# The first scale's weights by columns, and three conv tiles that run ahead of the shift

## The chip, the cores and the metric

One core of a Trainium2 chip runs the whole program once. The metric is the device time of that core in microseconds (us). PE is TensorE, DVE is VectorE, ACT is ScalarE, POOL is GpSimd, SP issues most of the transfers. A MiB is 128 partitions x 2048 fp32 words, the size of one weight tile.

## The reference

A decoder trunk of two layers over 256 tokens of width 1024. Only the head of its first layer matters here:

```python
c_act = jax.nn.silu(c)
sh1, sc1, g1, sh2, sc2, g2 = jnp.split(c_act @ ada_w[l] + ada_b[l], 6, axis=-1)
h = x * (1.0 + sc1[:, None, :]) + sh1[:, None, :]
# conv_module
a, g = jnp.split(h @ w_in + b_in, 2, axis=-1)
u = a * jax.nn.sigmoid(g)
u = depthwise_causal_conv(u, w_dw, taps=31) + b_dw
u = jax.nn.silu(layer_norm(u, g_n, b_n))
return u @ w_out + b_out
```

After it come the channel mixer (SwiGLU), the shared K/V projection, block-sparse attention and a mixture of eight experts, which make up most of the time and are not touched.

## The kernel before

Every fp32 product is made of three: each factor is split into a high and a low part (fp32r), and `mm3` (L198) adds high x high, high x low and low x high in PSUM. A weight tile is loaded (`load`, L165), its high part made by ACT (L189) and its low part by DVE, or by POOL for the names in `SPLIT_POOL` (L190).

The shift and the scale of the first layer are the two halves of one group of `ada_w`, `e00`. Each half is a product of the one row `c_act` (copied 32 times, `crep`) with a 1024x1024 matrix, in four row tiles of 1 MiB: `e00_w00` to `e00_w03` for the shift, `e00_w10` to `e00_w13` for the scale (`Ada.step`, L227). The result lies in rows, gets its bias from a broadcast load (`e00_b0`, L255), an add (L258), two transposes (L266) and a copy (L267), and is then a column per channel block: `c00c` for the scale, `c00h` for the shift.

The conv input projection has eight tiles of 256 output columns, `ci0` to `ci7`, in the order gate, value, gate, value; their PSUM tiles are `cip`. The program runs so:

- The scale half of `e00` and then `x` (token-major) are loaded; PE transposes `x` (`x_tr`, L325). `modulate` (L332) makes `hs` = x (1 + scale), without the shift, as a high and a low part.
- The first two tiles (`FIRST = 2`) multiply `hs`. What the shift adds to them is made separately: `shw` = shift x weights, 32 products into two rows (L519), copied (`shr`, L522), turned into columns by eight tiny products (L526) and added to the bias as `cin` (L530).
- The other six tiles multiply `h` = x (1 + scale) + shift (`hT`), made by a second `modulate`.
- From each pair of tiles ACT takes the sigmoid (`sg`, L588) and DVE makes `U` (L591), two blocks of 128 channels.
- The 31 taps of the eight channel blocks are divided: `CONV_VECTOR` on DVE (L548, five blocks and parts), `CONV_POOL` on ACT and POOL (blocks 1 and 3 whole and a part of 5: ACT multiplies, `pr`, L561, and POOL adds, L562, 70 adds), `CONV_TENSOR` on PE with diagonal matrices (`dg`, L476). DVE adds the parts of shared blocks (`dw`+`cp`, L612).
- The four tiles of the output projection, `cout`, have their low parts made by POOL (L190), behind its 70 adds. Then come the norm (L630 to L662) and the rest.

The order on each engine is that of a scheduler with a timeline of its own, which takes the program's instructions and their dependences; each engine's queue then runs in that order. SP's queue is the order of the loads.

Of the kernel before, what the change touches and what calls it, by code (L numbers as in the profile page):

```python
# [19 lines left out]
P = 128  # L20
D = 1024
# [50 lines left out]

CONV_VECTOR = (((0, 0, CK), (2, 0, CK)), ((4, 0, CK), (5, 11, CK), (7, 27, CK)))
FIRST = 2
SPLIT_POOL = ("ci2_0", "ci4_0", )
LN_ADD = ((1, 1),)
# [6 lines left out]
def build(ctx: ExitStack, tc: tile.TileContext, a: dict, dbg: dict | None = None):  # L85
# [92 lines left out]

    def split(raw, shape, name, spare=False, parts=1, gates=(), sub=None):
# [321 lines left out]
    wfirst = []
    for t in range(FIRST):
        if t:
            e00.fetch(0, 3)
        wfirst += colchunk(win, in_cols(t), 256, f"ci{t}", parts=1 if t else 2)
    c00h = ada_cols(e00.done(0), "c00h", sideps)
# [4 lines left out]
    psfirst = []  # L511
    for t in range(FIRST):
        psfirst.append(mmps(f"cip{t}"))
        dmajor([psfirst[-1]], wfirst[t:t + 1], hs)
# [12 lines left out]
    cin = small.tile([P, FIRST, 2], F32, tag="cin", name="cin", bufs=1)
# [56 lines left out]
    for ch in range(4):  # L584
# [701 lines left out]
```

## Time and profile before

| | |
|---|---|
| median of 3 runs | 1528.99 us (1527.67 to 1530.91) |
| the profiled execution | 1529.28 us |
| its span, first to last instruction | 1527.6 us |
| PE busy | 1469.6 us, 96% |
| DVE / ACT / POOL busy | 83% / 64% / 7% |
| granted TensorE clock, mean | 0.983 |

Busy time and spans are those of one profiled execution. The rows below show an engine's instructions in order of time: the start, the time from there to the end of the row's last instruction, the engine, the line, the output and its inputs, the shapes, how many, and in brackets how long the engine was idle before and what ended that. A clock of 1.00 is 2.4 GHz, 0.5 is 1.2 GHz.

### The profile page before, as it was taken

Reading aid. Unit: us, or ns where it says so; the run is one execution under the profiler, and the core shown is the slowest. Engines: PE = TensorE matmul, PEld = TensorE weight load, DVE = VectorE, ACT = ScalarE, POOL = GpSimd, SP = SyncE. Lnnn points to the kernel's source line nnn. Section 1 sums busy time; section 2 is a strip of 40 time slices with the busy share of each in tenths; the row PEclk is TensorE's granted clock in tenths of the full one; section 3 lists DMA queues with packets and bytes.
Section 4 is the critical chain, followed back from the end, with each engine's and each line's share of the span. In section 5 each row is a group of like instructions: output and inputs, shape, how many; then the busy total and the mean of one; then the engine's idle time right before and its main releaser. Section 6 shows DMA issues by size and latency. Waiting matters only on the chain. (4 is left out here: it accounts for less than half of the span.)

```text
span 1527.6 us, 20443 instructions
## 1 busy us (share of the span) xinstructions
PE 1469.6 (96%) x8042; PEld 1210.3 (79%) x8042; DVE 1264.0 (83%) x1260; ACT 985.0 (64%) x949; POOL 104.2 (7%) x101
## 2 busy tenths in 40 slices
PE   5995999999999999999999999999999999999995
PEld 3883798998976787888888888888888888887884
DVE  2897677756777799899889899988989988988886
ACT  5665444434656577777776776777767777667673
POOL 0696100001000100000000000000000000000000
PEclk9997999999999899999999999999999999999998
DMA  9765588865972688999999999999999999999991
GB/s 358 294 252 213 206 337 310 323 244 218 367 256 105 257 308 330 375 364 358 352 355 347 366 359 366 339 361 370 349 381 367 336 347 374 346 380 340 349 363 64
DMA packets 73380, 484.51 MB, mean 317 GB/s; under 512 B 9044, under 2 KB 11452, under 8 KB 17468
## 3 DMA queue, kind: packets, MB, share of 16 engines
q1 hardware_dynamic: 72848, 482.94, 84.1%
q8 instruction: 65, 1.06, 0.3%
q14 instruction: 39, 0.32, 0.1%
q10 hardware_dynamic: 428, 0.18, 0.0%
HBM read 482.04 MB, written 1.05 MB: 316 GB/s over the span
## 5 line engine op out<-in xcount | busy, mean ns | idle before, releaser
L190 DVE TENSOR_TENSOR eu_l<-eu,eu_h 128x2048 fp32r<-128x2048 f32 (+1 forms) x233 | 508.1, 2204 | 42.8 <-ACT eu_h L189 42.2
L189 ACT ACTIVATE eu_h<-eu 128x2048 fp32r<-128x2048 f32 (+1 forms) x233 | 425.7, 1848 | 100.4 <-PE eup L201 64.2
L202 PE MATMUL eup<-eu_l,g_x 128*128 128x512 f32 x896 | 353.8, 397 | 1.1 <-DVE eu_l L190 0.8
L200 PE MATMUL eup<-eu_h,g_x 128*128 128x512 f32 x896 | 350.4, 391 | 1.8 <-ACT eu_h L189 1.8
L201 PE MATMUL eup<-eu_h,g_x 128*128 128x512 f32 x896 | 349.8, 390 | 0.0
L190 DVE TENSOR_TENSOR e_l<-e,e_h 128x2048 fp32r<-128x2048 f32 (+1 forms) x114 | 251.0, 2212 | 25.8 <-ACT e_h L189 25.6
L189 ACT ACTIVATE e_h<-e 128x2048 fp32r<-128x2048 f32 (+1 forms) x114 | 210.2, 1854 | 21.5 <-PE eup L201 19.4
L202 PEld LDWEIGHTS eup<-eu_l,g_x 128*128 128x128 f32 x896 | 168.2, 188 | 43.2 <-DVE eu_l L190 9.5
L200 PEld LDWEIGHTS eup<-eu_h,g_x 128*128 128x128 f32 x896 | 168.3, 188 | 36.0 <-ACT eu_h L189 2.9
L201 PEld LDWEIGHTS eup<-eu_h,g_x 128*128 128x128 f32 x896 | 168.2, 188 | 35.7
L201 PE MATMUL eo<-e_h,egt 128*128 128x512 f32 x440 | 171.9, 391 | 0.0
L200 PE MATMUL eo<-e_h,egt 128*128 128x512 f32 x440 | 171.5, 391 | 0.0
L202 PE MATMUL eo<-e_l,egt 128*128 128x512 f32 x440 | 156.4, 397 | 0.0
L200 PEld LDWEIGHTS eo<-e_h,egt 128*128 128x128 f32 x440 | 82.6, 188 | 18.3 <-ACT e_h L189 0.4
L201 PEld LDWEIGHTS eo<-e_h,egt 128*128 128x128 f32 x440 | 82.6, 188 | 17.4
L202 PEld LDWEIGHTS eo<-e_l,egt 128*128 128x128 f32 x440 | 79.8, 188 | 15.5 <-issue 0.5
L1031 ACT ACTIVATE egt<-ept 128x512 fp32r<-128x512 f32 x56 | 33.2, 592 | 85.7 <-PE ept L1027 85.7
L1058 POOL TENSOR_TENSOR e_last_l<-e_last,e_last_h 128x1024 fp32r<-128x1024 f32 x1 | 3.0, 2994 | 988.3 <-ACT e_last_h L1056 988.3
L1023 ACT ACTIVATE es<-eup 128x512 f32<-128x512 f32 x56 | 33.3, 594 | 42.2 <-PE eup L202 41.9
L562 POOL TENSOR_TENSOR dw<-dw,pr 128x256 f32<-128x256 f32 x70 | 56.8, 814 | 5.1
L1024 DVE TENSOR_TENSOR eg<-es,eup 128x512 f32<-128x512 f32 x56 | 38.2, 683 | 17.6 <-PE eup L202 17.6
L227 PE MATMUL e_ps<-e_w,crep 128*32 128x256 f32 x576 | 43.8, 444 | 6.6 <-DMA e_w<-in_stream_dram 6.0
(400 smaller groups left out, 2424.1 us busy)
## 6 DMA issues: line engine op xcount, KB each, us to landing
eu<-in_stream_dram SPq DMA_DIRECT2D x216, 1024.0 KB, 6.8
e<-in_stream_dram SPq DMA_DIRECT2D x106, 1024.0 KB, 7.0
e_w<-in_stream_dram SPq DMA_DIRECT2D x46, 1024.0 KB, 6.1
fa<-in_stream_dram SPq DMA_DIRECT2D x11, 1024.0 KB, 6.0
fb<-in_stream_dram SPq DMA_DIRECT2D x11, 1024.0 KB
f<-in_stream_dram SPq DMA_DIRECT2D x11, 1024.0 KB, 7.2
ekv_w<-in_stream_dram SPq DMA_DIRECT2D x8, 1024.0 KB, 7.6
eu<-in_stream_dram SPq DMA_DIRECT2D x16, 512.0 KB, 6.5
```

The source lines that it names most:

```text
L189: ia = nc.scalar.activation(hi[:, ks], raw[:, ks], AF.Copy)
L190: iv = (sub or nc.vector).tensor_tensor(lo[:, ks], raw[:, ks], hi[:, ks].bitcast(F32), op=ALU.subtract)
L200: nc.tensor.matmul(out, lh, rh, start=start, stop=False)
L201: nc.tensor.matmul(out, ll, rh, start=False, stop=False)
L202: return nc.tensor.matmul(out, lh, rl, start=False, stop=stop)
L227: nc.tensor.matmul(self.ps[32 * g:32 * g + 32, h * 256:(h + 1) * 256], crep[:, 2 * q + j, :], raw[:, j, g * 256:(g + 1) * 256], start=(q = ...
L562: iv = nc.gpsimd.tensor_tensor(dw[:, i, :], dw[:, i, :], pr[:, j - b0, :], op=ALU.add)
L1023: nc.scalar.activation(s[:], pa[:], AF.Silu)
L1024: nc.vector.tensor_tensor(g[:], s[:], pb[:], op=ALU.mult)
L1031: ia = nc.scalar.activation(ghf, pt[:], AF.Copy)
L1058: (nc.gpsimd if (n, k0) == (1, 0) else nc.vector).tensor_tensor(lo[:, k0:k1], raw[:, k0:k1], hi[:, k0:k1].bitcast(F32), op=ALU.subtract)
```

## The change

The scale half of `e00` is loaded by columns: `load_scale(g)` takes the 256 columns of two channel blocks over all 1024 rows, 1 MiB, for g = 0 to 3. So one tile gives two finished blocks of the scale. Its 16 products write 64 rows each (`crep64`), the bias comes in by two loads on ACT's queue (`brow`), and an add (`sce`), one transpose (`sct`), and one step on DVE make two columns of A = 1 + scale. `x` comes channel-major from a second copy that the host lays out (`xch`), so PE's transposes are gone; ACT makes the high part of `hs` as A times `xch` and DVE the low part in one step. As soon as two blocks are there, the products of `cip0` with them can be made.

`FIRST` is 3: the tiles 0, 1 and 2 multiply `hs`, and `shw` has 48 products in two banks, with two copies and three adds. The shift's weights are fetched after `ci1` and `ci2`. `ci2` is split by DVE, `ci4` still by POOL but in four pieces. The token-major `x`, used later for the residual, is loaded behind the projection, into the buffer of `xch`.

```diff
-FIRST = 2
-SPLIT_POOL = ("ci2_0", "ci4_0", )
+FIRST = 3
+SPLIT_POOL = ("ci4_0", )
...
+    crep64 = act.tile([P, KB, 64], F32, tag="row", name="crep64", bufs=2)
+    nc.vector.tensor_copy(crep64[:], cact[:, :, None].to_broadcast([P, KB, 64]))
+    brow = tmp.tile([P, 4, P], F32, tag="g32", name="brow")
+    for u in range(2):
+        nc.scalar.dma_start(brow[64 * u:64 * u + 64, :, :], a["ada_b"][0, D:2 * D]
+                            .rearrange("(g m n) -> m g n", g=4, m=2)[u][None, :, :].to_broadcast([64, 4, P]))
...
             with after(*(gates[i] if gates else ())):
                 ia = nc.scalar.activation(hi[:, ks], raw[:, ks], AF.Copy)
-                iv = (sub or nc.vector).tensor_tensor(lo[:, ks], raw[:, ks], hi[:, ks].bitcast(F32), op=ALU.subtract)
+                for k0 in range(i * n, (i + 1) * n, cut or n):
+                    k1 = slice(k0, k0 + (cut or n))
+                    iv = (sub or nc.vector).tensor_tensor(lo[:, k1], raw[:, k1], hi[:, k1].bitcast(F32), op=ALU.subtract)
...
+    e00 = ada_group(0, 0, "e00")
+    xch = act.tile([P, KB, S], F32, tag="xtm", name="xch")
+    scps = sideps("sc_ps")
+    raws, wfirst = [], []
+    def load_scale(g):
+        raws.append(load(e00.w.tile(0, KB, D + g * 256, 256), [KB, 256], f"sc{g}", 2))
+    load_scale(0)
+    for u in range(2):
+        nc.sync.dma_start(xch[:, 4 * u:4 * u + 4, :], a[_CHANNELS][:, 4 * u:4 * u + 4, :])
+    raw0 = load(win.tile(0, KB, in_cols(0), 256), [KB, 256], "ci0_0", 2)
+    for g in range(1, 4):
+        load_scale(g)
...
-    e00.step(1, 3)
-    nc.sync.dma_start(xtm[:], a["x"][0].rearrange("(t p) d -> p t d", p=P))
-    e00.step(1)
-    xps = to_dmajor(xtm, "x")
-    c00c = ada_cols(e00.done(1), "c00c")
-    nc.vector.tensor_scalar(A[:], c00c[:], 1.0, None, op0=ALU.add)
-    _, (la, _) = modulate(xps, (A, None), "hs0", hs)
...
+    for g in range(4):
+        for k in range(KB):
+            for m in range(2):
+                nc.tensor.matmul(scps[64 * m:64 * m + 64, g * P:(g + 1) * P], crep64[:, k, :],
+                                 raws[g][:, k, m * P:(m + 1) * P], start=(k == 0), stop=(k == KB - 1))
+        e = small.tile([P, P], F32, tag="adae", name=f"sce{g}", bufs=2)
+        nc.vector.tensor_tensor(e[:], scps[:, g * P:(g + 1) * P], brow[:, g, :], op=ALU.add)
+        pst = mmps(f"sct{g}")
+        nc.tensor.transpose(pst[:, :P], e[:], ident[:])
+        nc.vector.tensor_scalar(A[:, 2 * g:2 * g + 2], pst[:, :P].rearrange("p (m r) -> p m r", m=2)[:, :, 0], 1.0, None,
+                                op0=ALU.add)
+        for k in (2 * g, 2 * g + 1):
+            la = nc.scalar.activation(hs_h[:, k, :], xch[:, k, :], AF.Copy, scale=A[:, k:k + 1])
+            lv = nc.vector.scalar_tensor_tensor(low(k), xch[:, k, :], A[:, k:k + 1], hs_h[:, k, :].bitcast(F32), op0=ALU.mult,
+                                           op1=ALU.subtract)
+        if g == 0:
+            wfirst.append(split(raw0, [KB, 256], "ci0_0", parts=2))
+        wh, wl = wfirst[0]
+        for k in (2 * g, 2 * g + 1):
+            for f in range(2):
+                fs = slice(f * P, (f + 1) * P)
+                im = mm3(psfirst[0][:, f * S:(f + 1) * S], (wh[:, k, fs], wl[:, k, fs]), (hs_h[:, k, :], low(k)),
+                    k == f == 0, k == KB - 1 and f == 1)
+    rawf = [load(win.tile(0, KB, in_cols(t), 256), [KB, 256], f"ci{t}_0", 2) for t in range(1, FIRST)]
+    e00.fetch(0)
+    for t in range(1, FIRST):
+        with after(la, lv):
+            wfirst.append(split(rawf[t - 1], [KB, 256], f"ci{t}_0", parts=2))
+        with after(im):
+            dmajor([psfirst[t]], wfirst[t:t + 1], hs)
...
+    xps = [xch[:, 2 * q:2 * q + 2, :].rearrange("p k s -> p (k s)") for q in range(KB // 2)]
...
-    psr = sideps("shw")
+    psr = [accps("shw0"), sideps("shw1")]
...
-    nc.vector.tensor_copy(shr[0:2, :], psr[0:2, :FIRST * 256])
+    nc.vector.tensor_copy(shr[0:2, 0:2, :], psr[0][0:2, :].rearrange("p (t c) -> p t c", t=2))
+    nc.vector.tensor_copy(shr[0:2, 2, :], psr[1][0:2, :256])
...
+    xtm = act.tile([P, NT, D], F32, tag="xtm", name="xtm")
+    nc.sync.dma_start(xtm[:], a["x"][0].rearrange("(t p) d -> p t d", p=P))
     for i, j0, j1 in CONV_POOL:
```

The order on the engines moves at these places. First SP's loads, from the conv tile `ci0` or `ci1` to the last piece of the shift's weights (`e00_w0x`). Before:

```order
L255 DMA e00_b1_209<-in_ada_b_dram 128x1x256
L173 DMA ci0_0_260<-in_stream_dram 128x1024 x2
L173 DMA e00_w00_269<-in_stream_dram 128x2048
L173 DMA e00_w01_271<-in_stream_dram 128x2048
L255 DMA e00_b0_316<-in_ada_b_dram 128x1x256
L173 DMA e00_w02_273<-in_stream_dram 128x2048
L173 DMA ci1_0_275<-in_stream_dram 128x2048
L173 DMA e00_w03_281<-in_stream_dram 128x1024 x2
```

After:

```order
L184 DMA ci1_0_331<-in_stream_dram 128x1024 x2
L184 DMA ci2_0_334<-in_stream_dram 128x1024 x2
L268 DMA e00_b0_503<-in_ada_b_dram 128x1x256
L268 DMA e01_b0_1330<-in_ada_b_dram 128x1x256
L184 DMA e00_w00_337<-in_stream_dram 128x2048
L184 DMA e00_w01_339<-in_stream_dram 128x2048
L184 DMA e00_w02_341<-in_stream_dram 128x2048
L184 DMA e00_w03_343<-in_stream_dram 128x1024 x2
```

The first shift tile is the seventh MiB before and the ninth after, and two bias broadcasts stand just ahead of it.

Second, PE's queue around the last shift products (`e00_ps`) and the products `shw`, after the change:

```order
L214 MATMUL cip2_176<-hs0_h_171,ci2_0_l_401 128x256
L215 MATMUL cip2_176<-hs0_l1_173,ci2_0_h_400 128x256
L240 MATMUL e00_ps_113<-e00_w02_341,crep_94 32x256 x8
L240 MATMUL e00_ps_113<-e00_w03_343,crep_94 32x256 x8
L279 MATMUL c00h_tr_508<-ident_80,e00_e0_505 128x128 x2
L568 MATMUL shw0_537<-ci0_0_h_202,shp_534 2x256
L568 MATMUL shw0_537<-ci0_0_l_203,shp_534 2x256
```

Before, the same shift products stood here:

```order
L202 MATMUL cip0_350<-hs0_l1_222,ci0_0_h_263 128x256
L227 MATMUL e00_ps_142<-e00_w02_273,crep_94 32x256 x8
L227 MATMUL e00_ps_142<-e00_w03_281,crep_94 32x256 x4
L200 MATMUL cip1_399<-hs0_h_220,ci1_0_h_277 128x256
L227 MATMUL e00_ps_142<-e00_w03_281,crep_94 32x256 x4
L201 MATMUL cip1_399<-hs0_h_220,ci1_0_l_278 128x256
```

They moved from ahead of `cip1` to behind `cip2`.

Third, DVE from the copy of `shw` to the first `U`, after the change:

```order
L571 COPY shr_587<-shw0_537 2x512
L203 TENSOR_TENSOR ci3_0_l_614<-ci3_0_611,ci3_0_h_613 128x2048
L353 CAST h0_h_512<-h0_f2_524 128x512
L572 COPY shr_587<-shw1_538 2x256
L353 CAST h0_h_512<-h0_f3_529 128x512
L355 TENSOR_TENSOR h0_l_513<-h0_f2_524,h0_h_512 128x512
L355 TENSOR_TENSOR h0_l_513<-h0_f3_529,h0_h_512 128x512
L582 TENSOR_TENSOR cin_596<-shw0_537,cols_133 128x2 x3
L203 TENSOR_TENSOR ci5_0_l_732<-ci5_0_729,ci5_0_h_731 128x2048
L643 SCALAR_TENSOR_TENSOR U_600<-cip1_175,cin_596,sg0_602 128x256 x2
```

and before:

```order
L342 TENSOR_TENSOR h0_l_326<-h0_f3_342,h0_h_325 128x512
L522 COPY shr_481<-shw_448 2x512
L190 TENSOR_TENSOR ci3_0_l_559<-ci3_0_556,ci3_0_h_558 128x2048
L530 TENSOR_TENSOR cin_487<-shw_448,cols_185 128x2 x2
L591 SCALAR_TENSOR_TENSOR U_490<-cip1_399,cin_487,sg0_492 128x256 x2
```

The split of `ci5` now stands ahead of `U`, and half of the `h` path's steps behind the copy. On ACT the high part of `ci6` moved in the same way, from behind the first eight `pr` to ahead of them.

## Rows read from the trace of the kernel before

**Rows 1.** Windows: length, busy PE, PEld, DVE, ACT, POOL; clock, DMA share, GB/s.

```profile
60.00:70.00 10.00, 10.00 (x89) 9.87 (x88) 9.40 (x15) 9.02 (x16) 9.37 (x10) 1.00 0.50 180
...
120.00:130.00 10.00, 0.01 (x1) 0.04 (x1) 6.73 (x6) 6.29 (x5) 9.76 (x6) 0.68 0.00 0
...
153.00:200.00 47.00, 46.63 (x365) 39.09 (x364) 30.98 (x47) 20.54 (x23) 3.87 (x3) 0.99 0.61 246
```

**Rows 2.** POOL's timeline; the last row is cut at 83 us.

```profile
44.61 4.61 POOL L190 TENSOR_TENSOR ci_l<-ci,ci_h 128x2048 fp32r<-128x2048 f32 x1 [41.69 <-ACT ci_h L189]
...
61.21 61.92 POOL L562 TENSOR_TENSOR dw<-dw,pr 128x256 f32<-128x256 f32 x70
123.09 18.47 POOL L190 TENSOR_TENSOR cout_l<-cout,cout_h 128x2048 fp32r<-128x2048 f32 x4
...
61.21 22.01 POOL L562 TENSOR_TENSOR dw<-dw,pr 128x256 f32<-128x256 f32 x20
```

**Rows 3.** DVE's timeline behind the convolution.

```profile
123.16 4.71 DVE L612 TENSOR_TENSOR dw<-dw,cp 128x256 f32<-128x256 f32 x1 [4.12 <-POOL dw L562]
...
137.65 3.93 DVE L355 TENSOR_TENSOR cn_w<-cn_w 128x2 f32<-128x2 f32 x1
141.61 0.16 DVE L356 TENSOR_TENSOR cn_w<-cn_w 128x2 f32<-128x2 f32 x1
```

**Rows 4.** PE's timeline, scale and shift products and the shift's transposes.

```profile
18.87 0.64 PE L227 MATMUL e_ps<-e_w,crep 128*32 128x256 f32 x8 [0.92 <-DMA e_w<-in_stream_dram]
...
30.01 1.07 PE L227 MATMUL e_ps<-e_w,crep 128*32 128x256 f32 x16
...
36.65 0.64 PE L227 MATMUL e_ps<-e_w,crep 128*32 128x256 f32 x8 [1.02 <-DMA e_w<-in_stream_dram]
...
42.03 0.38 PE L266 MATMUL c00h_tr<-ident,e_e 128*128 128x128 f32 x2
```

**Rows 5.** ACT's timeline.

```profile
9.00 9.16 ACT L476 ACTIVATE dg<-ident,dwT 128x128 f32<-128x128 f32 x31 [4.86 <-DMA rows<-in_conv_dw_b_dram]
21.88 1.06 ACT L189 ACTIVATE ci_h<-ci 128x1024 fp32r<-128x1024 f32 x1 [3.71 <-DMA ci<-in_stream_dram]
...
25.35 0.84 ACT L338 ACTIVATE hs_f<-x_tr,aff_A 128x256 f32<-128x256 f32 x2
...
58.41 0.60 ACT L556 ACTIVATE dw<-U,cols,dwT 128x256 f32<-128x256 f32 x1 [0.64 <-DVE U L591]
```

**Rows 6.** DVE's timeline ahead of the convolution.

```profile
20.88 0.42 DVE L258 TENSOR_TENSOR e_e<-e_ps,e_b 128x256 f32<-128x256 f32 x1 [14.78 <-DMA e_b<-in_ada_b_dram]
...
42.45 0.17 DVE L267 COPY c00h_c<-c00h_tr 128x8 f32<-128x8 f32 x1 [2.52 <-PE c00h_tr L266]
...
45.47 4.27 DVE L340 CAST h_h<-h_f 128x512 fp32r<-128x512 f32 x1 [2.45 <-ACT h_f L338]
...
50.38 0.42 DVE L340 CAST h_h<-h_f 128x512 fp32r<-128x512 f32 x1
50.83 0.69 DVE L342 TENSOR_TENSOR h_l<-h_f,h_h 128x512 fp32r<-128x512 f32 x1
...
53.74 0.67 DVE L522 COPY shr<-shw 2x512 f32<-2x512 f32 x1
54.48 2.29 DVE L190 TENSOR_TENSOR ci_l<-ci,ci_h 128x2048 fp32r<-128x2048 f32 x1
...
57.44 0.88 DVE L591 SCALAR_TENSOR_TENSOR U<-cip,cin,sg 128x256 f32<-128x256 f32 x2 [0.54 <-ACT sg L588]
```

**Rows 7.** Windows: of `cip` alone, of `shw` alone, and of all instructions (last two).

```profile
40.00:45.00 5.00, 5.00 (x42) 4.84 (x41) 0.00 (x0) 0.00 (x0) 1.00 1.00 413
...
45.60:49.20 3.60, 3.60 (x32) 2.57 (x31) 0.00 (x0) 1.00 1.01 420
...
19.70:26.50 6.80, 2.56 (x10) 1.98 (x10) 4.44 (x9) 4.29 (x8) 0.00 (x0) 0.61 1.01 413
122.20:135.60 13.40, 4.32 (x32) 2.48 (x36) 12.30 (x17) 4.84 (x5) 13.32 (x5) 0.55 0.33 125
```

More of the change, by code (lines that the diff above doesn't have):

```diff
@@ L44 @@
 TILES = 453
+_CHANNELS = "xt"
 class Weight:
@@ L71, in packed, with by_channel @@
     return out
+def by_channel(x):
+    return np.ascontiguousarray(x[0].T.reshape(KB, P, S).transpose(1, 0, 2))
 CONV_VECTOR = (((0, 0, CK), (2, 0, CK)), ((4, 0, CK), (5, 11, CK), (7, 27, CK)))
-FIRST = 2
-SPLIT_POOL = ("ci2_0", "ci4_0", )
+FIRST = 3
+SPLIT_POOL = ("ci4_0", )
 LN_ADD = ((1, 1),)
@@ L151, in build @@
     C_IN_B, C_DW_B, C_NG, C_NB, C_LNG, C_LNB = 0, 16, 24, 32, 40, 72
-    xtm = act.tile([P, NT, D], F32, tag="xtm", name="xtm")
     def columns():
@@ L177, in build, with split @@
     last_split, last_mm, last_norm, last_gt = [], [], [], []
-    def split(raw, shape, name, spare=False, parts=1, gates=(), sub=None):
+    def split(raw, shape, name, spare=False, parts=1, gates=(), sub=None, cut=0):
         if spare:
@@ L195, in wtile @@
         return split(load(src, shape, name, 1 if gates else parts), shape, name, spare, parts, gates,
-                     nc.gpsimd if name in SPLIT_POOL else None)
+                     nc.gpsimd if name in SPLIT_POOL else None, 2 if name in SPLIT_POOL else 0)
     def mm3(out, l, r, start, stop):
@@ L484, in build @@
+    for g in range(1, 4):
+        load_scale(g)
+    cols = columns()
     conv_diag(CONV_TENSOR[0][0], 0)
     conv_diag(CONV_TENSOR[0][0], 1)
-    e00 = ada_group(0, 0, "e00")
-    e00.step(1, 3)
-    nc.sync.dma_start(xtm[:], a["x"][0].rearrange("(t p) d -> p t d", p=P))
-    e00.step(1)
-    cols = columns()
-    xps = to_dmajor(xtm, "x")
-    c00c = ada_cols(e00.done(1), "c00c")
-    A = small.tile([P, KB], F32, tag="affA", name="aff0_A", bufs=4)
-    nc.vector.tensor_scalar(A[:], c00c[:], 1.0, None, op0=ALU.add)
@@ L496, in build @@
-    hs = (act.tile([P, KB, S], F32R, tag="big0", name="hs0_h"),
-          [tmp.tile([P, KB // 2, S], F32R, tag="gm", name=f"hs0_l{u}") for u in range(2)])
-    _, (la, _) = modulate(xps, (A, None), "hs0", hs)
-    with after(la):
-        conv_diag(CONV_TENSOR[1][0], 0)
[L501 to L506, printed above, removed]
+    A = small.tile([P, KB], F32, tag="affA", name="aff0_A", bufs=4)
@@ new lines, in build, with low @@
+    hs_h = act.tile([P, KB, S], F32R, tag="big0", name="hs0_h")
+    hs_l = [tmp.tile([P, KB // 2, S], F32R, tag="gm", name=f"hs0_l{u}") for u in range(2)]
+    psfirst = [accps(f"cip{t}") for t in range(FIRST)]
+    def low(k):
+        return hs_l[k // 4][:, k % 4, :]
+    for g in range(4):
[21 more added lines that the diff above has]
+                    k == f == 0, k == KB - 1 and f == 1)
@@ new lines, in build @@
+    hs = (hs_h, hs_l)
+    rawf = [load(win.tile(0, KB, in_cols(t), 256), [KB, 256], f"ci{t}_0", 2) for t in range(1, FIRST)]
[5 more added lines that the diff above has]
+            dmajor([psfirst[t]], wfirst[t:t + 1], hs)
+    with after(last_split[0]):
+        conv_diag(CONV_TENSOR[1][0], 0)
+    c00h = ada_cols(e00.done(0), "c00h")
+    xps = [xch[:, 2 * q:2 * q + 2, :].rearrange("p k s -> p (k s)") for q in range(KB // 2)]
@@ L510, in build @@
     ishp = nc.vector.tensor_tensor(shp[:, :, 1], c00h[:], shp[:, :, 0].bitcast(F32), op=ALU.subtract)
[L511 to L514, printed above, removed]
-    psr = sideps("shw")
+    psr = [accps("shw0"), sideps("shw1")]
     for t, (wh, wl) in enumerate(wfirst):
+        ps = psr[t // 2][0:2, t % 2 * 256:(t % 2 + 1) * 256]
         for k in range(KB):
             for u, w in enumerate((wh, wl)):
-                nc.tensor.matmul(psr[0:2, t * 256:(t + 1) * 256], shp[:, k, :], w[:, k, :], start=(t == k == u == 0),
-                                 stop=(t == FIRST - 1 and k == KB - 1 and u == 1))
-    shr = tmp.tile([P, FIRST * 256], F32, tag="g32", name="shr")
-    nc.vector.tensor_copy(shr[0:2, :], psr[0:2, :FIRST * 256])
-    psc = psr
-    for f in range(2 * FIRST):
-        nc.tensor.matmul(psc[:, f:f + 1], shr[0:2, f * P:(f + 1) * P], ones[0:2, 0:1], start=True, stop=True)
+                nc.tensor.matmul(ps, shp[:, k, :], w[:, k, :], start=(t % 2 == k == u == 0),
+                                 stop=((t % 2 == 1 or t == FIRST - 1) and k == KB - 1 and u == 1))
+    shr = tmp.tile([P, 4, 256], F32, tag="gm", name="shr")
+    nc.vector.tensor_copy(shr[0:2, 0:2, :], psr[0][0:2, :].rearrange("p (t c) -> p t c", t=2))
+    nc.vector.tensor_copy(shr[0:2, 2, :], psr[1][0:2, :256])
+    psc = psr[0]
+    for t in range(FIRST):
+        for f in range(2):
+            nc.tensor.matmul(psc[:, 2 * t + f:2 * t + f + 1], shr[0:2, t, f * P:(f + 1) * P], ones[0:2, 0:1],
+                             start=True, stop=True)
     cin = small.tile([P, FIRST, 2], F32, tag="cin", name="cin", bufs=1)
@@ L1278 @@
     args["stream"] = nc.dram_tensor("in_stream_dram", (TILES, P, 2048), F32, kind="ExternalInput").ap()
+    arrays["in_xt_dram"] = by_channel(inputs["x"])
+    args[_CHANNELS] = nc.dram_tensor("in_xt_dram", (P, KB, S), F32, kind="ExternalInput").ap()
     args["order"] = {}
```

## The prediction, made before the changed kernel ran

> **What bounds the kernel now.** I read the stages first (busy time in windows), then the timelines of POOL, DVE, ACT and PE there, last the instruction orders. From 153 us on PE is busy for 46.63 of 47.00 us at clock 0.99 [rows 1], it holds 96% of the span, and both programs then have the same order. So the change can only move the point at which that stretch begins, and a shift there passes through one to one: the row shows PE full and the transfers at 0.61 of their time.
>
> What sets that point is not PE. Between 120 and 130 us PE works 0.01 us [rows 1]. The reader should see in POOL's timeline why: 70 adds of the depthwise convolution run without a break from 61.21 for 61.92 us, to 123.09, and four splits of `cout` follow for 18.47 us [rows 2]. DVE waits 4.12 us for the last add, and then its small operations each last as long as one POOL split: the 128x256 add takes 4.71 us, a 128x2 one 3.93; the next 128x2 one, behind the last split, 0.16 [rows 3]. So **the time of POOL's first add, the 62 us and the 18.5 us behind them** are the path. The first add waits for ACT's first `pr`, that for `U`, that for `cin`, that for the products `shw` of the shift, from 45.60 us [rows 7]; those wait for the shift itself. I cost these in turn.
>
> **1. When the shift products start.** The change turns the front round: scale first, shift late. In PE's queue, which is in order, the products of the first MiB of shift weights (`w00`) now stand ahead of the last four products of `cip0`, those of `w01` inside `cip1`, those of `w02` and `w03` behind all of `cip2`. All four stood ahead of the bulk of `cip1`. So `shw` now starts at a sum: arrival at `w00`, then everything PE still has to do.
>
> *Arrival at `w00`.* It is the ninth MiB of the big loads. The fifth was used at 18.87 us, the product of the eleventh's first half (10.5 MiB) at 36.65 [rows 4]: 3.2 us per MiB, so 9 MiB give 31.8, and two new 0.25 MiB loads of the bias `brow` 0.6 to 1.6 more: **33**, an estimate from these two rows. It cannot be below PE's own arrival. ACT makes the 31 diagonals from 9.00 for 9.16 us, then two halves of `ci0` at 1.06 [rows 5]: 21 to 21.6. Then four pairs of blocks, each through an add (0.42), a transpose (0.38), a copy (0.17), two activations (0.84) and one low part (0.44 for a 128x256 with three operands) [rows 4 to 6]: 2.3 us each, in sequence 30.8; overlapped, down to 28.
>
> A small broadcast can land late here: the add of the first shift-and-scale bias began at 20.88 us and waited for it, when the last products before it had ended at 19.51 [rows 4, 6]. In SP's order two such broadcasts, `e00_b0` and `e01_b0`, now go out just ahead of `w00`; before, they stood behind it. If each holds `w00` back by the 1.4 us of that wait, `w00` lands at 35.8. I leave this out of the sum, since `w00` need only follow them in the queue, not wait for them, and price it as a rival. The Trainium skill (DMA: Bandwidth & Descriptors, Rules for kernel authors) speaks for it: a transfer whose outermost dimension counts a few rows is confined to that many of the 16 DMA engines, and these broadcasts go out as four, so four engines would have to finish them before their part of `w00`. No row here shows the engines apart.
>
> *From there.* Four products of `cip0` and 48 each of `cip1` and `cip2`: 100 at 5.00 / 42 = 0.119 us, 11.9 us [rows 7]. The 32 shift products: 16 take 1.07 us [rows 4], so 2.1. Both at full clock. A clock below full costs more: 19.70 to 26.50 us, with PE busy 2.56 of 6.80 us, had 0.61 [rows 7], between the levels of 1.2 and 2.4 GHz, and 40 to 45, all busy, 1.00. Waits for the pairs and for `w00` make the first pattern likely again. I take 2 us, between 0 and 5: a stretch of 10 us at half speed loses 5, and the longest here with a clock near half is 13.4 us [rows 7]. Then add, transpose, copy, two `shp` steps and gaps: 0.42 + 0.38 + 3 x 0.17 + 0.5 = 1.8 [rows 4, 6]. Sum 33 + 11.9 + 2.1 + 2 + 1.8 = 50.8 against 45.60: **+5.2**. Ends: arrival 28, full clock gives 43.8 (-1.8); 33 with 5 us of half clock gives 53.8 (+8.2).
>
> **2. From the shift to the first add.** Before: 61.21 - 45.60 = 15.6 us [rows 2, 7]. After, along DVE's order: 32 `shw` products for the first bank 3.6 [rows 7], the copy of 2x512 0.67, the split of `ci3` 2.29, two casts of 0.42, a second copy about 0.4, two low parts at 0.69, three adds for `cin` 0.3, then the split of `ci5`, now ahead of `U`, 2.29, and `U` 0.88 [rows 6]: 12.7. ACT adds `dw` 0.60, the high part of `ci6`, which now stands ahead of `pr`, about 2.0 as two halves, and one `pr` 0.42 [rows 5]: 15.7, with small waits 15.9, that is +0.3. The 16 further `shw` products of the third tile (1.8 us) lie beside the split of `ci3`. Added is only POOL's split of `ci4`, in four pieces of 4.61 / 4 = 1.15 us [rows 2], which now lies beside this DVE chain. Before, POOL's split of `ci2` held a cast there for 4.27 us instead of 0.42 [rows 6], beside `shw`, so taking it away returns little: 0.4. Each piece can hold one DVE operation by up to 1.15: nothing to 3.4 (one piece starts alone). I take 1.7, the middle. Term: **+2.0**, from +0.3 to +3.7.
>
> **3. POOL's chain.** Before, the DVE splits of `ci5`, `ci6` and `ci7` fall among the first 20 adds: these take 22.01 us, the other 50 take 39.9, 0.80 each, so a split costs (22.01 - 16.0) / 3 = 2.0. Of three there stay two (`ci6`, `ci7`), since `ci5` has gone ahead: **-2.0** [rows 2]. If `ci5` slides back beside the adds: 0.
>
> **4. Behind it.** Four `cout` splits of POOL still hold DVE's operations one by one, 18.5 us; fewer DVE operations are left there, so one split may be free: 0, or -4.6.
>
> **At nothing.** `x` is loaded a second time (1 MiB) behind the first weights of the next group; transfers there take 0.50 of their time [rows 1]. Without that cover 1 MiB is 3.2 us, and its first reader comes behind the norm, after 141 us [rows 3]. The 16 transposes of `x` go, at a time when PE waited for loads. One tile fewer goes through the `h` path: 48 products, 5.7 us of PE, at a time when PE is ahead of POOL.
>
> **Sum:** +5.2 + 2.0 - 2.0 = +5.2 on the profiled execution, 1529.28 (span 1527.6 and some 1.7 around it), which is 0.3 above the median 1528.99: **1534.5**. Measurement tells about 0.2%, 3.1 us, from no change.
>
> **The rivals.**
> *The loads come early (faster).* If `w00` has landed when PE gets there and the pairs overlap, PE arrives at 28, stays at full clock, and the pieces hold nothing: -1.8 + 0.3 - 2.0 = -3.5, **1525.8**. For it: the products start with the first scale weights, and PE was idle for 4.2 of 6.8 us from 19.70 [rows 7]. Against it: ACT cannot have `ci0` before 21, and 8 MiB stand in the queue ahead of `w00`. The point: a first add before 61. With a free split in part 4 as well it is 1521. Chance 0.16.
> *It evens out (same).* Arrival 31 and full clock, pieces hold nothing: 46.8, +1.2 + 0.3 - 2.0 = -0.5 at the least; with a short half clock of 2 us, +1.5: about **1530**. Also the forecast with a free split in part 4: 1529.9. Together 0.26.
> *Late behind the broadcasts (worse).* `w00` at 35.8 instead of 33, all else as forecast: +2.8, **1537.3**. For it: the 20.88 us add. Against it: that add needs the broadcast itself, `w00` does not. It decides if `w00`'s product starts past 34. Chance 0.12.
> *A long half clock (worse).* 53.8 and all pieces holding: +8.2 + 3.7 - 2.0 = +9.9, **1539**. For it: PE waits several times between 22 and 33 in short turns, and two stretches of that kind had 0.61 and 0.55 [rows 7]. Chance 0.14.
>
> **How the numbers follow.** The forecast has 0.32 (1532.4 to 1536.5). The slower side is 0.32 + 0.12 + 0.14 = 0.58, same 0.26, faster 0.16. The range reaches into the faster rival (1521 to 1525.9), of which some 0.07 stay below it, and past the worse one, with some 0.08 above: 1523 to 1540.
>
> **What would show it.** Right: `e_ps<-e_w` waiting for its load near 33 us; no 4.27 us cast; `shw` starting near 50.8; the first add at 66 to 67; 60 us of adds; last add near 128; PE idle longer before 135. Wrong: the first add before 61, which would show step 1 failed; adds of over 62 us (step 3); a tail other than 18.5 us behind the last add (step 4); or a stretch behind 153 us in which PE no longer passes the shift through.

## The result, and the profile after

The changed kernel takes 1543.93 us (median of 4 runs, 1541.34 to 1547.23) where the kernel before, beside it, took 1529.95 (4 runs, 1527.67 to 1533.33): ratio 1.0092, 95% interval 1.0076 to 1.0109. It is **slower by 14 us**. The sign was forecast, the size was not: 1534.5 was expected, and 1543.93 lies past the upper end, 1540. The profiled execution of the changed kernel took 1541.34 (span 1539.6), the fastest of its four; that of before took 1529.28, so these two traces differ by 12.1 only. A second trace of each, from the last part of the experiments, stands beside them here. All numbers are starts in us:

| | before | changed | before, 2nd | changed, 2nd |
|---|---|---|---|---|
| ACT's diagonals `dg` | 9.00 | 14.09 | 9.26 | 14.87 |
| first `cip` product | 24.67 | 25.59 | 24.44 | 26.38 |
| first product of the shift weights (`e_ps`, `w00`) | 26.89 | 37.18 | 26.65 | 40.67 |
| first `shw` product | 45.60 | 55.12 | 47.39 | 59.84 |
| POOL's first add | 61.21 | 71.21 | 61.85 | 75.83 |
| first `dw<-dw,cn_rows` behind the norm | 143.86 | 155.59 | 144.61 | 160.07 |
| first evacuation of the output projection (`xh`) | 166.01 | 174.32 | 164.66 | 178.80 |
| from there to the end | 1361.5 | 1365.3 | 1365.2 | 1365.9 |

The second pair shows the whole loss in front: +12.4 at `shw`, +14.1 at `xh`, and 0.7 behind. In the first pair 8.3 of 12.1 us lie in front, and the last row of the table, which was shortest in the first trace of before, makes the rest. In the other runs below it lies between 1363.4 and 1367.8, hardly further apart than the two traces of before (3.6): it is taken as a part that varies by itself, though no run isolates it.

POOL's timeline answers to [rows 2]. Its adds begin 10.00 us later and take 2.0 less; the splits behind them are as before.

```profile
62.89 8.21 POOL L203 TENSOR_TENSOR ci_l<-ci,ci_h 128x512 fp32r<-128x512 f32 x4 [11.03 <-ACT ci_h L200]
71.21 59.91 POOL L614 TENSOR_TENSOR dw<-dw,pr 128x256 f32<-128x256 f32 x70
131.07 18.10 POOL L203 TENSOR_TENSOR cout_l<-cout,cout_h 128x2048 fp32r<-128x2048 f32 x4
```

ACT's timeline answers to [rows 5]. The two `brow` loads are issued first; of the six small loads behind them in ACT's queue the third goes out at 7.92, the fourth at 12.83 and the last at 13.55, and the diagonals follow that one, 5.09 us later than before. Both halves of `ci0` stand behind the diagonals.

```profile
1.42 0.70 ACTq L148 DMA_DIRECT2D brow<-in_ada_b_dram  x1
...
3.86 0.60 ACTq L148 DMA_DIRECT2D brow<-in_ada_b_dram  x1
...
7.92 0.28 ACTq L156 DMA_DIRECT2D rows<-in_conv_norm_g_dram  x1
12.83 0.28 ACTq L156 DMA_DIRECT2D rows<-in_conv_norm_b_dram  x1
...
13.55 0.43 ACTq L156 DMA_DIRECT2D rows<-in_ln_b_dram  x1
14.09 9.16 ACT L489 ACTIVATE dg<-ident,dwT 128x128 f32<-128x128 f32 x31 [10.05 <-DMA rows<-in_conv_norm_g_dram]
23.15 1.99 ACT L200 ACTIVATE ci_h<-ci 128x1024 fp32r<-128x1024 f32 x2
```

The same loads in the kernel before, with no `brow`:

```profile
4.29 0.31 ACTq L143 DMA_DIRECT2D rows<-in_conv_norm_g_dram  x1
4.64 0.31 ACTq L143 DMA_DIRECT2D rows<-in_conv_norm_b_dram  x1
...
8.57 0.32 ACTq L143 DMA_DIRECT2D rows<-in_ln_b_dram  x1
```

PE's timeline answers to [rows 4]. From the first `cip` product on, PE works through its queue with short waits (the largest below is 2.16, ahead of that product). The row to see is 37.18: the shift's products begin **with no wait for their load**.

```profile
25.59 0.39 PE L213 MATMUL cip<-hs_h,ci_h 128*128 128x256 f32 x1 [2.16 <-ACT hs_h L536]
...
28.05 1.52 PE L527 MATMUL sc_ps<-sc,crep 128*64 128x128 f32 x22
...
35.75 0.39 PE L213 MATMUL cip<-hs_h,ci_h 128*128 128x256 f32 x1 [0.79 <-ACT hs_h L536]
...
37.18 1.07 PE L240 MATMUL e_ps<-e_w,crep 128*32 128x256 f32 x16
```

`w00` is the first of the five loads of the shift's weights. It was issued at 22.02 and landed 13.6 us later, at 35.6, so it was there 1.6 us ahead of PE. SP's timeline, then the times from issue to landing (the 13.6 is that of `w00`):

```profile
22.02 13.07 SPq L184 DMA_DIRECT2D e_w<-in_stream_dram  x5
```

```profile
e_w<-in_stream_dram SPq DMA_DIRECT2D x3, 1024.0 KB, 13.6
```

Windows of PE from the first `cip` product to the first `shw` product (us, PE busy, clock, DMA share, GB/s), of all instructions, of `cip`, of `e_w` and of `sc_ps`:

```profile
25.59:55.12 29.53, 26.18 (x244) 1.00 0.88 326
25.59:55.12 29.53, 19.32 (x144) 1.00 0.88 326
25.59:55.12 29.53, 4.08 (x64) 1.00 0.88 326
25.59:55.12 29.53, 2.61 (x32) 1.00 0.88 326
```

The stretch of the kernel before that corresponds, of all instructions:

```profile
24.67:45.60 20.93, 18.56 (x162) 0.92 1.02 388
```

PE has 82 instructions and 7.6 us of work more there: 48 `cip` products of the third tile, 32 products of the scale that still stand behind the first `cip` product. In this trace the clock was full all the while, so none of it is lost to half speed.

### The profile page after: what moved, and what is told of

Its sections match the earlier page's. It is cut to its first block, busy times and chain, and to the rows that moved or that the text cites. A ratio compares the mean times of both kernels' runs of the same rounds, so it can differ in the third digit from the quotient of the medians.

```text
span 1539.6 us, 20607 instructions
## 1 busy us (share of the span) xinstructions
PE 1473.3 (96%) x8112; PEld 1218.1 (79%) x8112; DVE 1265.9 (82%) x1271; ACT 985.2 (64%) x951; POOL 100.8 (7%) x103
## 5 line engine op out<-in xcount | busy, mean ns | idle before, releaser
L213 PEld LDWEIGHTS eo<-e_h,egt 128*128 128x128 f32 x440 | 83.0, 189 | 18.5 <-ACT e_h L200 0.6
L1078 DVE TENSOR_TENSOR eg<-es,eup 128x512 f32<-128x512 f32 x56 | 38.4, 685 | 17.6 <-PE eup L215 17.6
L214 PE MATMUL fap<-h_h,fa_l 128*128 128x256 f32 x176 | 48.8, 279 | 0.5 <-DVE fa_l L203 0.5
```

The source lines that it names most:

```text
L213: nc.tensor.matmul(out, lh, rh, start=start, stop=False)
L214: nc.tensor.matmul(out, ll, rh, start=False, stop=False)
L1078: nc.vector.tensor_tensor(g[:], s[:], pb[:], op=ALU.mult)
```

## The experiments

The theories they are to part: the loss is made **by ACT's late start** (the `brow` loads ahead of the small ones); **by the transfer of `w00`**, behind the broadcasts `e00_b0` and `e01_b0`; **by PE's own queue**, longer by a tile; or **by PE's clock**. No kernel below leaves out any of the computation.

**ACT's start alone.** The `brow` loads move behind the loop of the small ones:

```
-    brow = tmp.tile([P, 4, P], F32, tag="g32", name="brow")
-    for u in range(2):
-        nc.scalar.dma_start(brow[64 * u:64 * u + 64, :, :], ...)
     rows = tmp.tile([104, P], F32, tag="h32", name="rows")
...
         off += n
+    brow = tmp.tile([P, 4, P], F32, tag="g32", name="brow")
+    for u in range(2):
+        nc.scalar.dma_start(brow[64 * u:64 * u + 64, :, :], ...)
```

> The changed kernel with the two bias loads brow issued behind the six small rows loads on ACT's queue. Theory (ACT is late): in the changed kernel ACT's diagonals started at 14.09 us instead of 9.00, behind rows loads that were issued only when a brow load had landed, and PE reached the first shift products at 37.18. Then the diagonals start at 9 to 10.5, the first shift products come at 32 to 34, shw 18 us later (50 to 52 instead of 55.1), the first POOL add at 66 to 68 instead of 71.2. The two cn_rows products also stand together again in this order, which by the theory on the end of the stage gives another 3 to 4 us: 1534 to 1538 us in all. Rival (the transfer is late): the first shift tile was issued at 22.0 and took 13.6 us to land, 35.6; PE waits for it, shw starts at 53.5, and the front gives back 1.6 us only.

1543.42 us, ratio 1.0103 (1.0081 to 1.0125): no gain. The diagonals start at 10.66 instead of 14.09, but DVE's first add of the scale now waits for `brow`, and PE for that add. DVE's and PE's rows:

```profile
20.80 0.29 DVE L530 TENSOR_TENSOR sce<-sc_ps,brow 128x128 f32<-128x128 f32 x1 [6.15 <-DMA brow<-in_ada_b_dram]
```

```profile
21.14 0.47 PE L532 MATMUL sct<-ident,sce 128*128 128x128 f32 x1 [6.80 <-DVE sce L530]
```

The two broadcasts of 128 KB, issued from 9.19, are there at 20.80. The first `cip` product comes at 25.16 and the shift's products at 35.34, 1.8 us earlier than in the changed kernel, but `shw` at 56.17, 1.0 later: in this order 108 `cip` products stand behind the first shift products instead of 100, and one of the shift's products waits 0.80 for its load. So the edit moved the wait and did not part the theories; `brow` has to go, not to move.

**No `brow` at all.** The bias comes as eight rows of one more small load, through the transpose that makes `cols`, and is added behind the scale's transpose:

```
-    rows = tmp.tile([104, P], F32, tag="h32", name="rows")
+    rows = tmp.tile([112, P], F32, tag="h32", name="rows")
...
+    nc.scalar.dma_start(rows[104:112, :], a["ada_b"][0, D:2 * D].rearrange("(k p) -> k p", p=P))
...
-        nc.vector.tensor_tensor(e[:], scps[:, g * P:(g + 1) * P], brow[:, g, :], op=ALU.add)
+        nc.vector.tensor_copy(e[:], scps[:, g * P:(g + 1) * P])
...
-        nc.vector.tensor_scalar(A[:, 2 * g:2 * g + 2], ..., 1.0, None, op0=ALU.add)
+        nc.vector.scalar_tensor_tensor(A[:, 2 * g:2 * g + 2], ..., 1.0,
+                                       cols[:, 104 + 2 * g:106 + 2 * g], op0=ALU.add, op1=ALU.add)
```

> The changed kernel without the bias broadcasts brow: the scale's bias comes as eight more rows of the small rows load (4 KB) and is added behind the transpose. Theory (PE's queue): ACT's diagonals start at 9 to 10.5 us instead of 14.1, the first product of cip0 at 22 to 24 instead of 25.6, and from there PE works through the same queue of some 27 us almost without a wait, so shw starts at 50 to 52 and the first add comes at 66 to 68: 1536 to 1540 us. Rival (the transfer of the first shift tile at 35 us binds): shw stays at 54 to 56 and the time within 2 us of the changed kernel.

1538.81 us, ratio 1.0065 (1.0046 to 1.0083): 4 to 5 us of the 14 are gone. The profiled execution, 1535.34, is the fastest of its four (the others: 1538.68 to 1539.17), so its starts are those of a fast one. The diagonals start at 9.42, the first `cip` product at 21.81, `shw` at 49.84, the first add at 65.82, 5.4 earlier than in the changed kernel. Now, and only now, the shift's products wait for `w00`:

```profile
32.80 0.42 PE L237 MATMUL e_ps<-e_w,crep 128*32 128x256 f32 x4 [0.83 <-DMA e_w<-in_stream_dram]
```

`w00` itself lands earlier too, at 32.7 (issued at 20.41, 12.3 us) instead of 35.6. So this run takes away both delays of `brow`, that of ACT and that of the transfer.

**The broadcasts behind `w00`.** In the changed kernel, and then in the one without `brow`, the shift biases of `e00` and `e01` are issued behind the last weight load:

```
-            nc.sync.dma_start(bias[:], ...)
+            with after(*(last_load if (self.name, h) in (("e00", 0), ("e01", 0)) else ())):
+                nc.sync.dma_start(bias[:], ...)
```

> The changed kernel with the two bias broadcasts e00_b0 and e01_b0 issued behind the shift's weights instead of just ahead of them. Theory (ACT is late): the first shift tile lands earlier than 35.6 us, by 2 to 4 us, but PE gets to its products at 37 as before; shw at 55, first add at 71, no gain in the front (within 1 us). Rival (the transfer is late): shw and the first add come 1.5 to 4 us earlier. At the end of the stage the order differs a little (16 products of the next group ahead of both cn_rows), which may give or take 2 us.

> The kernel without brow, and with the broadcasts e00_b0 and e01_b0 behind the shift's weights. Theory (PE's queue): as without brow alone, within 1.5 us. Rival (the transfer binds once ACT is early): shw 2 to 4 us earlier than without brow alone, at 47 to 50, and the time 2 to 4 us lower.

In the changed kernel: 1544.19, ratio 1.0098 (1.0081 to 1.0116), the shift's products at 37.27 where they were at 37.18, again with no wait for their load: the transfer is not what PE waits for there. `shw` (57.09) and the first add (73.08) come 1.9 to 2.0 us later than in the first trace of the changed kernel: the diagonals start 0.8 later, the clock was 0.58 from 28 to 32 us, and 108 `cip` products stand behind the first shift products instead of 100. Without `brow`: 1536.5, ratio 1.0050 (1.0034 to 1.0066); the products start at 31.38 with no wait, `shw` at 49.01, 0.8 earlier than with the broadcasts ahead.

```profile
31.38 1.07 PE L237 MATMUL e_ps<-e_w,crep 128*32 128x256 f32 x16
...
49.01 0.28 PE L566 MATMUL shw<-ci_h,shp 128*2 128x256 f32 x1 [0.67 <-DVE shp L560]
```

So the broadcasts do hold `w00`, but their price is 1.4 us at the shift's products and 0.8 at `shw` (2.3 by the medians; the profiled execution with the broadcasts ahead was a fast one), and ACT's late start hid it. The Trainium skill (DMA: Bandwidth & Descriptors, Rules for kernel authors) has the rule that a transfer with a few outermost rows runs on at most as many DMA engines; by it `w00` could be held behind these broadcasts. The wait agrees, 0.83 us with them ahead and none with them behind, but no row shows the engines apart.

**The third tile.** `FIRST` back to two, in the changed kernel and in the last one:

```
-FIRST = 3
+FIRST = 2
...
-    nc.vector.tensor_copy(shr[0:2, 2, :], psr[1][0:2, :256])
```

> The changed kernel with FIRST = 2 again (two tiles ahead of the shift; the copy of the third is left out), all else as changed. Theory (PE's queue between the first shift products and shw is the delay): 48 products of 0.119 us fewer stand there, shw starts 5 to 6 us earlier (49 to 50), the first add comes 4 to 6 us earlier (65 to 67), the time falls by 4 to 9 us with the order at the end of the stage. Rival: loads of the shift's weights or ACT bound that place, and shw moves by less than 2 us.

> The same with FIRST = 2. Theory (PE's queue): 48 products of 0.119 us less ahead of shw, which starts at 44 to 47, about where it started before the change (45.6); the first add at 60 to 63, the time 1526 to 1533 us, level with the kernel before: the whole loss is then PE's work put ahead of shw. Rival (something else of the change costs, such as the second load of x or the pieces on POOL): the first add is level with before but the time stays over 1535 us.

The first: 1537.62, ratio 1.0055 (1.0037 to 1.0072); `shw` 4.1 us earlier, 51.01. The second: 1530.15, ratio 1.0007 (0.9997 to 1.0017), level with the kernel before, `shw` at 42.38, 6.6 earlier than with three tiles. By the medians the third tile costs 6.3 us in both. In both the first add follows POOL's pieces of `ci4` directly: ACT's first `pr` was done at 65.19 and 56.67, the pieces at 67.80 and 57.02, and the adds began at 67.75 and 56.98. So the pieces hold the adds by some 2.6 us in the first and 0.3 in the second. POOL's rows of the second:

```profile
51.67 5.35 POOL L200 TENSOR_TENSOR ci_l<-ci,ci_h 128x512 fp32r<-128x512 f32 x4 [12.56 <-ACT ci_h L197]
56.98 61.98 POOL L611 TENSOR_TENSOR dw<-dw,pr 128x256 f32<-128x256 f32 x70
```

The early start is worth 4.2 us there against before (first add 56.98, not 61.21), and 3.7 at `xh` (162.34); of that the median shows nothing. Behind `xh` this trace took 1365.4, that of before 1361.5 and 1365.2, so part of it can be the varying remainder; where the rest went stays open.

**The join behind the norm.** In the changed kernel the two pairs of `cn_rows` products have the 32 products of `e02` between them, PE's rows:

```profile
149.96 1.22 PE L705 MATMUL cn_rows<-cn_dg,ones 128*128 128x256 f32 x2 [9.56 <-DVE cn_dg L693]
151.11 3.64 PE L240 MATMUL e_ps<-e_w,crep 128*32 128x256 f32 x32
154.68 0.88 PE L705 MATMUL cn_rows<-cn_dg,ones 128*128 128x256 f32 x2
```

The edit moves the block `e02`/`e01` ahead of the norm's coefficients and orders these behind it:

```
+    with after(*trs):
+        e01.step(1)
+        e01_1 = e01.done(1)
+        e02.step(0, 2)
     mv = small.tile([P, NT, 2], F32, tag="cnmv", name="cn_mv", bufs=1)
...
-    rc = rstd_of(mv[:, :, 1], "cn", n=NT)
+    with after(e01.last):
+        rc = rstd_of(mv[:, :, 1], "cn", n=NT)
```

> The changed kernel with the add of the second group's bias (e_e) put ahead of the norm's small steps on DVE, as before the change, so that the products of the third group stand ahead of both cn_rows and run while POOL splits. Theory (order at the join): the first dw<-dw,cn_rows starts 1.5 to 3 us behind the norm's last step instead of 6.4 us, the front is as in the changed kernel (first add 71.2), and the time falls by 3 to 4.5 us, to 1539 to 1541. Rival: the moved add is held by one more POOL split (4.4 us) and nothing is gained; or the stage behind hides it.

1544.5, ratio 1.0101 (1.0082 to 1.0120): no gain. All four `cn_rows` products now stand together, and the first `dw` product follows the norm's diagonals by 2.65 us (153.96 to 156.61) instead of 6.17 (149.42 to 155.59):

```profile
154.49 2.08 PE L706 MATMUL cn_rows<-cn_dg,ones 128*128 128x256 f32 x4 [7.26 <-DVE cn_dg L699]
156.50 1.93 PE L240 MATMUL e_ps<-e_w,crep 128*32 128x256 f32 x16
```

The run's own front was 4.4 us later than in the first trace of the changed kernel (first add 75.58), like the second trace; against that second trace `xh` comes 1.1 us earlier. The 32 products have to be done in any case.

**Second traces.** Both kernels once more, with no edit:

> The kernel before once more, unchanged, for a second trace. From the first DVE step on the output projection (xh, 166.0 us in the first trace) to the end the first trace took 1361.6 us; the changed kernel and all eight variants so far took 1364.8 to 1366.7 there, with the same order of instructions. Theory (the later part varies by itself, with the clock granted there, and the first trace of before was at the low end): this trace shows 1363 to 1367 us for that part, or a first add or xh at another place than 61.2 and 166.0. Rival (the change costs 4 us behind 166 us as well): it shows 1361 to 1362 again.

> The changed kernel once more, unchanged, for a second trace: its first trace was of the fastest of four executions (1541.34 us; median 1543.93). Theory (what varies is the clock granted to PE while it works in short turns between 16 and 46 us): the time is 1543 to 1546 us, a stretch of PE's work there is at 0.5 to 0.7 of the clock, shw starts 2 to 4 us later than 55.1, and the part from xh to the end takes 1364 to 1367 us as in the first trace. Rival (the difference lies elsewhere): shw at 55 to 55.5 and the extra time behind the first add.

1531.63 and 1546.39, one execution each. The changed kernel's front is 4.6 us later than in its first trace, and PE's clock is the main reason. Windows of its second trace, then of its first (us, PE busy, clock, DMA share, GB/s):

```profile
28.00:32.00 4.00, 4.00 (x28) 0.50 1.04 304
40.00:44.00 4.00, 4.00 (x29) 0.58 0.64 231
```

```profile
28.00:32.00 4.00, 4.00 (x44) 1.00 1.02 305
40.00:44.00 4.00, 4.00 (x41) 1.00 0.98 397
```

In the same stretch of the same program PE is always busy and works 28 instructions at half clock (1.2 GHz), or 44 at full (2.4). The front of the changed kernel can come out either way, `shw` at 55.12 or 59.84; of the 4.7 us between, 0.8 is there already at ACT's diagonals.

**POOL's splits of `cout`.** Step 4 of the prediction left them at 18.5 us. The first try, on the kernel before, cuts each in four:

```
-            wout.append(split(raw, [2, D], f"cout{q}", q == 3, sub=nc.gpsimd))
+            wout.append(split(raw, [2, D], f"cout{q}", q == 3, sub=nc.gpsimd, fine=4))
```

> The kernel before the change with each of POOL's four cout splits cut into four pieces of 128x512. Theory (a whole POOL split holds DVE's next step): with pieces DVE gets in after at most some 1.2 us each, the norm's last step ends at 129 to 133 us instead of 141.8, PE's cn_rows come 8 us earlier, and the time falls by 5 to 10 us, to 1519 to 1525. Rival (the stage is bound by POOL's splits themselves, or by loads that wait for them): the norm ends early, but the first products with cout wait for the low parts or for loads, and less than 3 us is gained.

1532.99, ratio 1.0018 (1.0005 to 1.0031): no gain, perhaps a small loss. A step held for 4 us before is now held for 1.2, but more of them are held, and the 16 pieces take 20.02 us instead of 18.47. DVE's rows:

```profile
136.57 1.18 DVE L360 SCALAR_TENSOR_TENSOR cn_w<-cn_w 128x2 f32<-128x2 f32 x1
137.79 2.47 DVE L641 TENSOR_SCALAR cn_dg<-ident,cn_w 128x128 f32<-128x128 f32 x2
...
141.45 2.47 DVE L644 TENSOR_SCALAR cn_dg<-ident,cn_rn 128x128 f32<-128x128 f32 x2
```

Then the low parts of `cout` are taken off POOL and done by DVE, behind the norm's last small step, on the kernel before and on the best of the kernels above:

```
-            wout.append(split(raw, [2, D], f"cout{q}", q == 3, sub=nc.gpsimd))
+            hl = ...
+            nc.scalar.activation(hl[0][:], raw[:], AF.Copy)
+            wout.append((hl[0], hl[1], raw))
...
+    with after(idg):
+        for q in range(KB // 2):
+            h, l, r = wout[q]
+            nc.vector.tensor_tensor(l[:], r[:], h[:].bitcast(F32), op=ALU.subtract)
+            wout[q] = h, l
```

> The kernel before with the low parts of the four cout tiles made by DVE behind the norm's small steps instead of by POOL beside them. Theory (POOL's splits hold DVE's steps one by one): the norm's last step comes at 128 to 132 us instead of 141.8, four splits of 2.3 us follow on DVE (9.2), the first dw<-dw,cn_rows comes at 139 to 141 instead of 143.9, the output projection starts 3 to 6 us earlier: 1523 to 1527 us. Rival (loads of the next group, which wait for the splits to free their buffers, bind): PE waits for them behind cn_rows and the time is within 2 us of before.

> The changed kernel without brow, with the broadcasts behind the shift's weights, with FIRST = 2, and with the low parts of cout made by DVE behind the norm's small steps. The front alone (without the last edit) had its first add at 57.0 us and 1530.2 us in all. Theory: last add at 118 to 120, the first dw<-dw,cn_rows at 134 to 137 instead of 143.1, 1521 to 1526 us, under the kernel before and the changed one. Rival (the join hides it): the gain of the front and of the splits is given back in waits for loads, and the time is 1527 us or more.

On the kernel before: 1528.71, ratio 0.9987 (0.9975 to 0.9998), a gain of 2 us and less than expected. On the other: **1524.07, ratio 0.9948 (0.9932 to 0.9965), faster than both kernels of this case**. In the first of the two the norm's last small step stands at 131.59 where it was at 141.81, the four low parts take 8.89 us instead of 18.47, and the `dw` products begin 2.3 us earlier. DVE's rows of the second:

```profile
124.62 0.15 DVE L369 SCALAR_TENSOR_TENSOR cn_w<-cn_w 128x2 f32<-128x2 f32 x1
...
125.79 8.89 DVE L700 TENSOR_TENSOR cout_l<-cout,cout_h 128x2048 fp32r<-128x2048 f32 x4
134.60 0.68 DVE L721 TENSOR_TENSOR dw<-dw,cn_rows 128x512 f32<-128x512 f32 x1
```

Its first add is at 57.96 and `xh` at 154.85, 11.2 us ahead of the first trace of before; 1367.8 behind `xh`, the longest of all, give part of it back.

## Why the sign was right and the size wrong

**Step 1, the shift's start: this is the one that failed.** It gave `shw` at 50.8, +5.2; it came at 55.12, +9.5, and at 59.84 in the second trace. The step's sum had two parts. *From `w00` on*, 17.8 us were forecast and 17.94 measured (37.18 to 55.12), by two errors that cancel: the shift's 64 products took 4.08, since 16 stand behind each MiB and not 8 as counted, and the 2 us of half clock did not come in that trace.

*The arrival at `w00`* was put at 33 and was 37.18. The place that failed is the sentence that costs `brow` by its bytes, 0.6 to 1.6, in the transfer of `w00`, beside one that leaves ACT's diagonals at 9.00. The loads stand in ACT's queue ahead of six small ones, the diagonals stand behind these and start at 14.09, and ACT has `ci0` at 25.1 (23.15 + 1.99) where the sum had 21 to 21.6. Also left out of PE's own arrival were the 32 products of the scale behind the first `cip` product (2.61). With these two the four pairs give 25.1 + 9.2 + 2.6 = 37.0, close to what came.

The transfer was under-priced as well: `w00` landed at 35.6, 2.6 past the 33, though the `brow` loads are 128 KB each, half of what the sum took. But PE came later still, and a load that is there earlier changes nothing then, as the run with the broadcasts behind `w00` shows.

The runs without `brow` show it: with ACT at 9.42 and 9.50 the arrival is 32.80 and 31.38, and `shw` 49.84 and 49.01, 1.0 and 1.8 ahead of the 50.8 of the sum. The run with `brow` moved comes nearest to ACT early with the load late (diagonals at 10.66, `w00` landed at 35.1): its shift products start at 35.34, so without an earlier load not much more than 1.8 us of the arrival comes back, and the earlier load is part of what leaving `brow` out gained.

**The half clock** was put at 2 us, between 0 and 5. It was 0 in the first trace and is most of the 4.7 us by which `shw` came later in the second; the median, 1543.93, lies between the two executions (1541.34 and 1546.39). So the rival with 0.14, a long half clock, is what happened in some executions, on top of ACT's delay. ACT's delay, with full clock from the first `cip` product on, gave 1541.34; no run shows the half clock without ACT's delay.

**The rivals.** The late broadcast was right in its mechanism, and its 35.8 close to the 35.6 at which `w00` landed, but it had no effect in the changed kernel, since PE came later still. Its sign, products past 34, is there for another reason. The wait near 33 that was to show the forecast right is not there, and its absence is the sign that the bound was PE's queue behind ACT. The faster one, with the loads early, needed PE at `w00` by 28; even without `brow` and broadcasts it came at 31.38.

**Step 2, from the shift to the first add:** 16.1 measured (55.12 to 71.21), 17.6 forecast, 15.6 before. The chain to `pr` was right, `ci5` ahead of `U` and `ci6` ahead of `pr`: 15.9 forecast without the pieces, 16.0 measured. But the 15.6 of before is not this chain. There POOL split `ci4` whole from 56.32 to 61.25, and the first add stood behind that; ACT's first `pr` was done at 59.42, 1.8 us earlier. So the path of the prediction, a first add that waits for `pr`, does not hold in the kernel before: the chain to `pr` grew by 2.2 us and the first add moved by 0.5. Rows of before, POOL's and then ACT's:

```profile
56.32 4.93 POOL L190 TENSOR_TENSOR ci_l<-ci,ci_h 128x2048 fp32r<-128x2048 f32 x1 [6.86 <-ACT ci_h L189]
```

```profile
58.92 3.30 ACT L561 ACTIVATE pr<-U,dwT 128x256 f32<-128x256 f32 x8
```

In the changed kernel the pieces of `ci4` held DVE by nothing like the 1.7 assumed: beside them DVE's two low parts (0.64 each), the three adds for `cin` and the split of `ci5` take 1.27, 0.29 and 2.80 us, the last 0.51 more than [rows 6] have, and it is POOL's pieces that last longer, 8.21 us for the four instead of 4.93 for the whole. The last piece (71.11) and ACT's first `pr` (71.13) end together, 0.1 us ahead of the first add. DVE's rows, then two of POOL's, then ACT's:

```profile
62.86 1.27 DVE L355 TENSOR_TENSOR h_l<-h_f,h_h 128x512 fp32r<-128x512 f32 x2
64.31 0.29 DVE L582 TENSOR_TENSOR cin<-shw,cols 128x2 f32<-128x2 f32 x3 [0.17 <-PE shw L577]
64.64 2.80 DVE L203 TENSOR_TENSOR ci_l<-ci,ci_h 128x2048 fp32r<-128x2048 f32 x1
```

```profile
65.25 3.34 POOL L203 TENSOR_TENSOR ci_l<-ci,ci_h 128x512 fp32r<-128x512 f32 x1
...
69.81 1.30 POOL L203 TENSOR_TENSOR ci_l<-ci,ci_h 128x512 fp32r<-128x512 f32 x1
```

```profile
70.63 3.29 ACT L613 ACTIVATE pr<-U,dwT 128x256 f32<-128x256 f32 x8
```

**Step 3, the adds:** −2.0 forecast, 61.92 to 59.91 measured. Right.

**Step 4, the tail:** the splits took 18.10. Right. But "both programs then have the same order" was too broad: the join put 32 products between the `cn_rows` pairs, so the `dw` products came 11.7 us later where the norm came 7.4 later (149.22, not 141.81). Most of it was work done early: at `xh` the difference was 8.3. Setting it right returned about 1 us at `xh`, and no time that the median shows.

**Passing through one to one:** the second pair has it, +14.0 at the first add, +14.1 at `xh`, +14.8 at the end. The first pair has +10.0, +8.3 and +12.1: the two traces of before differ by 2.1 us between the `dw` products and `xh` (22.15 and 20.05), and by 3.6 the other way behind it. Over all traces here `xh` lies between 154.85 and 178.80, and the time behind it between 1361.5 and 1367.8, so a shift of the front does pass through, but one pair of traces tells it to some 4 us only.

## What to carry to other kernels

When a front is turned round, write down the arrival of every engine anew and follow each queue from its first entry: here two loads of 128 KB, placed first in ACT's queue, put off that engine's work behind the small loads by 5 us, which a price by their bytes did not show. A start that comes earlier is worth only what the awaited engine then has left to do: here a third tile on PE took 6.3 us, more than starting by pairs gave. An edit that gives nothing alone can give something once another wait is gone: the place of the broadcasts was worth nothing in the changed kernel and 0.8 us at `shw` without `brow`. With the loads, the broadcasts and the tile all out of the way the front was 4 us earlier than before.

## What was not expected of the hardware

- The same program had PE's clock at 0.50 and at 1.00 in the same busy stretch (28 to 32 us) in two executions. The front of the kernel then varies by 4.7 us at `shw`, nearly the 5.2 that the forecast gave to the whole change.
- Holding between POOL and DVE goes both ways. Beside POOL's 128x2048 splits a 128x2 step of DVE takes 3.93 us [rows 3]; beside splits cut in 128x512 it takes 1.2, and a 128x128 one the same (0.16 and 0.24 unhindered). In the changed kernel two of POOL's pieces, beside DVE's low parts and its 128x2048 split (64.64 to 67.44), took 2.40 and 3.34 us, the other two 1.30. Finer pieces shared the delay out and took none away; moving the work to DVE, where a part takes 2.2 us instead of 4.6, did.
- Two broadcasts of 128 KB on ACT's queue were issued from 9.19 us and there only at 20.80, while the big loads ran; ahead of the small loads they put off ACT's work by 5.09.
